# Where the weights of the sixth of seven products are loaded to, in two woven matmul pairs

## The chip, the cores and the metric

The kernel runs on one core of one Trainium2 chip. Its time is device time in microseconds (us), the median of three runs. A profile of one execution, taken by the hardware profiler, is read beside it.

## The reference

Two layers on x of 256 tokens by 2048 channels, in float32: an even one (a linear recurrent unit beside dilated attention) and an odd one (gated linear attention beside a spatial gating unit), then a norm. What matters here is the odd layer's input projection:

```
h = rms_norm(x, norm)
z = h @ w_in                       # 2048 x 7184
q, k, v, a_lr, gc, u, vd, gd = split(z)
yc = rms_norm(gla_chunked(q, k, v, log_a), head_norm) * silu(gc)
yd = spatial_gating(gelu(u), gelu(vd), w_s, b_s, v_norm) * silu(gd)
x = x + concat(yc, yd) @ w_out
```

Every column block of z of 512 columns is a product of 256 x 2048 with 2048 x 512.

## The kernel before, in words

**Products.** float32 values are split in two parts, hi (a cast to float32r on ScalarE, line 138) and lo (the rest, by a subtraction on VectorE, line 73), and each product is three matmuls: hi x hi, hi x lo, lo x hi. A piece of weights of 128 x 1024 (512 KB) comes by one DMA into a buffer, is cast into whi (four buffers) and subtracted into wlo (four buffers), and feeds TensorE. Once the subtraction has run, the raw buffer is free, if nothing else reads it.

**Rings.** Raw buffers come in three rings: `raw` with three buffers, `rx` and `ry` with four each (line 115). Outside the pairs every piece takes the next of the rings in a fixed turn. While `paired[0]` is set, a piece of the stream goes into `raw` alone.

**Pairs.** Two column blocks and two halves of the tokens are a 2 x 2 by 2 x 2 block product over the two halves of the inner dimension. `pair` computes it with seven block products of half size in place of eight. Each is four steps; a step takes one piece and runs six matmuls of 512 columns. Two chains of pieces, x0 (in `rx`) and y0 (in `ry`), are used again and again, changed in place between uses: GpSimd issues DMAs that add other weights to them (line 244). The products run in this order: m12 with x0, m3 with y0, m56 with x0, m7 with y0, m56 again with x0 (the fifth), then the sixth, which adds to m12 and takes four fresh pieces z0, and the seventh, m4, with x0 to which VectorE has added z0 (line 295). In a short loop of six rounds the sixth and seventh products run two rounds apart. The weights z0 are fetched in that loop, into `raw`. In it each z0 buffer stays in use until line 295 has read it.

**Stream.** `weave` puts steps of other products (gates, gd, vd: `Stream`) between the steps of a pair, 14 steps into the first pair (q and k) and 12 into the second (the two blocks of u). A stream step is one piece and twelve matmuls. A task queue (`spawn`, `tick`) feeds the small work of attention, norms and gates in between.

**Queues.** SyncE issues the plain loads in order; an issue that waits for a buffer holds those behind it. The order on each queue is set by the framework's scheduler at build time, from the program's order and the buffers, so a piece's issue may stand far ahead of its use. In the names below a number tells the tiles of one ring apart.

Of the kernel before, what the change touches and what calls it, by code (L numbers as in the profile page):

```python
# [51 lines left out]
def trunk(ctx, tc, x, xt, lead, w_in0, w_out0, w_va, w_in1, w_out1, w_gate, small, dist, cst, w_alpha, w_s,  # L52
# [31 lines left out]
    def mid_tile(shape, name, dtype=F32):  # L84
        return mid.tile(shape, dtype, name=name, tag="mid")
# [13 lines left out]
    def tick(n):  # L99
        for task in list(tasks):  # L100
            task[1] -= n
            if task[1] <= 0:
                wait = next(task[0], None)
                if wait is None:
                    tasks.remove(task)
                else:
                    task[1] = wait
# [11 lines left out]
    def raw_tile(shape, tag=None):  # L119
        if tag is None:  # L120
            tag = "raw"
            if not paired[0]:
                turns.append(turns.pop(0))
                tag = turns[-1]
        return rawp.tile(shape, F32, name=tag, tag=tag, bufs=rings[tag])
# [9 lines left out]
    def parts(raw, n=1024):  # L135
        hi = hip.tile([P, n], F32R, name="whi", tag="whi")
        lo = lop.tile([P, n], F32R, name="wlo", tag="wlo")
        nc.scalar.copy(hi, raw)  # L138
        sub(lo, raw, hi)
        return hi, lo  # L140
# [68 lines left out]
    def piece_of(w, u, i):  # L209
        return w[u + i // 2][:, i % 2 * 1024:i % 2 * 1024 + 1024]  # L210

    def fetch(w, u, i, tag):
        raw = raw_tile([P, 1024], tag)
        nc.sync.dma_start(out=raw, in_=piece_of(w, u, i))
        return raw
# [14 lines left out]
    def pair(w, ua, ub, act, forms, x0, tag):  # L230

        f3, f5, f6, f7 = forms

        def step(ps, a, i, raw, first, u=None):  # L240
            tile_, k0, b = a
            hi, lo = parts(raw)
            if u is not None:
                nc.gpsimd.dma_start(out=raw, in_=piece_of(w, u, i), accum_op=ALU.add)
            for kk in range(2):
                j = 2 * i + kk
                wh, wl = hi[:, kk * 512:(kk + 1) * 512], lo[:, kk * 512:(kk + 1) * 512]
                xh = tile_[:, k0 + j, b * P:(b + 1) * P]
                xl = tile_[:, k0 + j, T + b * P:T + (b + 1) * P]
                nc.tensor.matmul(ps, xh, wh, start=(first and j == 0), stop=False, skip_group_check=not first)  # L250
                nc.tensor.matmul(ps, xh, wl, start=False, stop=False, skip_group_check=not first)  # L251
                nc.tensor.matmul(ps, xl, wh, start=False, stop=(j == 7), skip_group_check=not first)  # L252
                tick(1)

        def run(ps, a, raws, first, u=None):
            for i, raw in enumerate(raws):
                step(ps, a, i, raw, first, u)
                yield

        def bank():  # L260
            return psm.tile([P, 512], F32, name="ps", tag="ps")

        m12, m3, m56, m7 = bank(), bank(), bank(), bank()
        y0 = []
        for i, raw in enumerate(x0):
            y0.append(fetch(w, ub + 2, i, tag))
            step(m12, (act, 0, 0), i, raw, True, ub)
            yield
        s1 = mid_tile([P, 512], "s1")
        nc.scalar.copy(s1, m12)  # L270
        yield from run(m3, f3, y0, True, ub)
        yield from run(m56, f5, x0, True, ub + 2)
        s5 = mid_tile([P, 512], "s5")
        nc.scalar.copy(s5, m56)
        yield from run(m7, f7, y0, True)
        yield from run(m56, f6, x0, False)
        t = mid_tile([P, 512], "t")
        nc.vector.tensor_tensor(out=t, in0=m56, in1=s1, op=ALU.subtract)
        c22 = s1
        nc.vector.tensor_tensor(out=c22, in0=m7, in1=t, op=ALU.add)  # L280
        nc.vector.tensor_tensor(out=t, in0=m3, in1=t, op=ALU.add)
        nc.vector.tensor_tensor(out=s5, in0=s5, in1=c22, op=ALU.subtract)
        m4 = bank()
        z0 = []
        for i in range(6):
            if i < 4:
                z0.append(fetch(w, ua + 2, i, "raw"))
                step(m12, (act, 8, 0), i, z0[i], False)
                yield
            if i > 1:  # L290
                step(m4, (act, 8, 1), i - 2, x0[i - 2], True)
                yield
            if 0 < i < 5:

                tc.keep_in_program_order(nc.vector.tensor_tensor(out=x0[i - 1], in0=z0[i - 1], in1=x0[i - 1],
                                                                 op=ALU.add))
        nc.vector.tensor_tensor(out=s5, in0=m4, in1=s5, op=ALU.add)
        return [m12, s5], [t, c22]
# [528 lines left out]
    paired[0] = True  # L827
    x0 = [fetch(w_in1, 6, i, "rx") for i in range(4)]
    ps, ps_k = weave(pair(w_in1, 6, 10, act2, forms2, x0, "ry"), stream, 14)
    drain()  # L830
    eb, enb, ebl = decays
# [129 lines left out]
    paired[0] = True  # L961
    x0 = [fetch(w_in1, 30, i, "rx") for i in range(4)]
    ud = weave(pair(w_in1, 30, 34, act2, forms2, x0, "ry"), stream, 12)
    paired[0] = False
    for c, ps in enumerate(ud):
# [52 lines left out]
    for s in range(4):  # L1018
        raw = raw_tile([P, 4, 256])
# [118 lines left out]
```

## Time and profile before

| | |
|---|---|
| time, median of 3 runs | 886.4 us (885.5 to 886.6) |
| time of the profiled execution | 889.86 us |
| its span | 888.2 us |
| TensorE busy | 864.7 us, 97% |
| VectorE busy | 590.4 us, 66% |
| ScalarE busy | 513.0 us, 58% |
| mean granted clock of TensorE | 0.99 |

In the names of the profile PE is TensorE, DVE is VectorE, ACT is ScalarE, POOL is GpSimd and SPq is SyncE's queue of DMA issues. Times on the axis count from the span's start. A matmul's duration is longer than the distance to the next one's start, since matmuls are pipelined; the distance of starts tells the rate. The first pair stands at about 539 to 628 us, the second at about 686 to 779.

### The profile page before, as it was taken

To read this page: it belongs to the slowest core of one execution; us is meant where nothing else is said; L and a number is where in the kernel's file an instruction comes from. 1 tells how busy PE (TensorE), PEld (TensorE's weight loads), DVE (VectorE), ACT (ScalarE), POOL (GpSimd) and SP (SyncE) were. 2 spreads that over 40 slices of the span, in tenths; PEclk is the share of its full clock that TensorE was granted. 3 is DMA by queue.
4 is the path that set the end of the run, shared out by engine and by line. 5 is a ranking of instruction groups with operands and counts; after the bars stand their busy time and mean duration, and the time that the engine had idled before them with its cause. 6 is when DMAs were issued, how large, how long until landed. Compare 5 with 4: busy or idle time off the path is not lost.

```text
span 888.2 us, 11858 instructions
## 1 busy us (share of the span) xinstructions
PE 864.7 (97%) x4432; PEld 728.7 (82%) x4432; DVE 590.4 (66%) x848; ACT 513.0 (58%) x751; POOL 31.0 (3%) x48
## 2 busy tenths in 40 slices
PE   8999999999999999999999999997999998899996
PEld 7888888888888888888888988885867886688886
DVE  7577557677576587666555995677645868695652
ACT  6765456676766766554444775653535765564532
POOL 0000000000000000010000002200000220000000
PEclk9999999999999999999999999998999999999999
DMA  9796555555455455565545669965733996665502
GB/s 342 288 389 212 189 192 164 169 174 173 161 178 166 143 181 173 190 210 193 189 127 157 209 199 205 267 218 166 254 127 120 199 266 221 194 232 186 192 3 96
DMA packets 49114, 171.35 MB, mean 193 GB/s; under 512 B 5520, under 2 KB 6032, under 8 KB 48800
## 3 DMA queue, kind: packets, MB, share of 16 engines
q1 hardware_dynamic: 44496, 154.75, 51.2%
q0 software_dynamic: 4416, 15.76, 8.7%
q8 instruction: 35, 0.57, 0.3%
q14 instruction: 23, 0.19, 0.1%
q10 hardware_dynamic: 144, 0.07, 0.0%
HBM read 168.47 MB, written 2.10 MB: 192 GB/s over the span
## 4 chain that ended last, share of the span: by engine, by line
PE 93%; DMA 3%; DVE 2%; ACT 1%; issue 0%; ACTq 0%
PE pc L311 20%; PE ps L146 16%; PE ps L147 16%; PE ps L148 16%; PE pc L310 10%; DMA raw<-in_w_in 3%; PE ps L250 2%; PE ps L252 2%; PE ps L251 2%; DVE wlo L73 1%; PE pc L313 1%; ACT whi L138 1%; PE sc L496 1%; PE gp L580 1%; PE gp L579 1%; DMA sm<-in_small 0%
## 5 line engine op out<-in xcount | busy, mean ns | idle before, releaser
L311 PE MATMUL pc<-act,whi 128*128 128x512 f32 x768 | 269.6, 395 | 0.0
L310 PE MATMUL pc<-act,wlo 128*128 128x256 f32 x720 | 208.7, 290 | 0.0
L73 DVE TENSOR_TENSOR wlo<-rx,whi 128x1024 fp32r<-128x1024 f32 (+2 forms) x117 | 140.3, 1201 | 79.6 <-ACT whi L138 78.5
L138 ACT CAST whi<-rx 128x1024 fp32r<-128x1024 f32 (+1 forms) x114 | 118.8, 1044 | 93.4 <-PE ps L148 55.4
L311 PEld LDWEIGHTS pc<-act,whi 128*128 128x128 f32 x768 | 142.8, 188 | 29.2
L146 PE MATMUL ps<-whi,act 128*128 128x512 f32 (+2 forms) x416 | 159.4, 386 | 5.7 <-ACT whi L138 4.5
L73 DVE TENSOR_TENSOR wlo<-ry,whi 128x1024 fp32r<-128x1024 f32 (+2 forms) x101 | 120.8, 1198 | 66.1 <-ACT whi L138 65.5
L73 DVE TENSOR_TENSOR wlo<-raw,whi 128x1024 fp32r<-128x1024 f32 (+2 forms) x98 | 116.9, 1193 | 62.2 <-ACT whi L138 60.7
L147 PE MATMUL ps<-wlo,act 128*128 128x512 f32 (+2 forms) x416 | 157.7, 379 | 0.3 <-DVE wlo L73 0.3
L148 PE MATMUL ps<-whi,act 128*128 128x512 f32 (+2 forms) x416 | 157.3, 378 | 0.0
L138 ACT CAST whi<-raw 128x1024 fp32r<-128x1024 f32 (+1 forms) x95 | 98.6, 1038 | 93.3 <-PE ps L148 37.9
L138 ACT CAST whi<-ry 128x1024 fp32r<-128x1024 f32 (+1 forms) x99 | 102.8, 1039 | 84.1 <-PE ps L148 52.6
L310 PEld LDWEIGHTS pc<-act,wlo 128*128 128x128 f32 x720 | 136.0, 189 | 2.5 <-DVE wlo L73 0.9
L146 PEld LDWEIGHTS ps<-whi,act 128*128 128x128 f32 x416 | 78.9, 190 | 23.9 <-ACT whi L138 6.1
L146 PE MATMUL ps<-whi,yt 128*128 128x512 f32 (+1 forms) x256 | 97.4, 380 | 0.0
L148 PE MATMUL ps<-whi,yt 128*128 128x512 f32 (+1 forms) x256 | 96.5, 377 | 0.0
L147 PE MATMUL ps<-wlo,yt 128*128 128x512 f32 (+1 forms) x256 | 96.3, 376 | 0.0
L148 PEld LDWEIGHTS ps<-whi,act 128*128 128x128 f32 x416 | 79.3, 191 | 14.4
L147 PEld LDWEIGHTS ps<-wlo,act 128*128 128x128 f32 x416 | 79.4, 191 | 14.1 <-DVE wlo L73 0.7
L148 PEld LDWEIGHTS ps<-whi,yt 128*128 128x128 f32 x256 | 48.2, 188 | 8.9
L147 PEld LDWEIGHTS ps<-wlo,yt 128*128 128x128 f32 x256 | 48.3, 189 | 8.4
L146 PEld LDWEIGHTS ps<-whi,yt 128*128 128x128 f32 x256 | 48.2, 188 | 8.4
(288 smaller groups left out, 923.8 us busy)
## 6 DMA issues: line engine op xcount, KB each, us to landing
raw<-in_w_in SPq DMA_DIRECT2D x76, 512.0 KB, 4.9
ry<-in_w_in SPq DMA_DIRECT2D x66, 512.0 KB, 4.8
rx<-in_w_in SPq DMA_DIRECT2D x66, 512.0 KB, 4.5
rx<-in_w_out SPq DMA_DIRECT2D x23, 512.0 KB, 4.6
ry<-in_w_out SPq DMA_DIRECT2D x23, 512.0 KB, 4.6
raw<-in_w_out SPq DMA_DIRECT2D x18, 512.0 KB, 4.6
rx<-in_w_in POOLq DMA_DIRECT2D x16, 512.0 KB, 9.7
ry<-in_w_in POOLq DMA_DIRECT2D x8, 512.0 KB, 9.7
```

Of the source, the lines that this page charges most:

```text
L73: nc.vector.tensor_tensor(out=o, in0=a, in1=hi.bitcast(F32), op=ALU.subtract)
L138: nc.scalar.copy(hi, raw)
L146: nc.tensor.matmul(ps[b], xh, wh, start=first, stop=False)
L147: nc.tensor.matmul(ps[b], xh, wl, start=False, stop=False)
L148: nc.tensor.matmul(ps[b], xl, wh, start=False, stop=last)
L250: nc.tensor.matmul(ps, xh, wh, start=(first and j == 0), stop=False, skip_group_check=not first)
L251: nc.tensor.matmul(ps, xh, wl, start=False, stop=False, skip_group_check=not first)
L252: nc.tensor.matmul(ps, xl, wh, start=False, stop=(j == 7), skip_group_check=not first)
L310: nc.tensor.matmul(ps[c][:, 1, :], wl, act[:, k, 0:T], start=False, stop=False)
L311: nc.tensor.matmul(ps[c], wh, act[:, k, :], start=(k == 0), stop=(k == KT - 1))
L313: nc.tensor.matmul(ps[c][:, 1, :], wl, act[:, k, 0:T], start=False, stop=False)
L496: nc.tensor.matmul(sc[:, 1:3, :], qk[:, 0, P:T], qk[:, 1, :], start=True, stop=True)
```

## The change

The four fetches of z0 move from the last loop (sixth and seventh product) into the fifth product, one ahead of each of its steps, and their tag is the second chain's ring, `ry`, in place of `raw`. Nothing is computed otherwise. Line numbers grow by 5 for the sums behind the fifth product and by 3 from the additions of line 295 on.

```
--- before.py
+++ after.py
@@ -273,7 +273,12 @@
         s5 = mid_tile([P, 512], "s5")
         nc.scalar.copy(s5, m56)
         yield from run(m7, f7, y0, True)
-        yield from run(m56, f6, x0, False)
+
+        z0 = []
+        for i, raw in enumerate(x0):
+            z0.append(fetch(w, ua + 2, i, tag))
+            step(m56, f6, i, raw, False)
+            yield
         t = mid_tile([P, 512], "t")
         nc.vector.tensor_tensor(out=t, in0=m56, in1=s1, op=ALU.subtract)
         c22 = s1
@@ -281,10 +286,8 @@
         nc.vector.tensor_tensor(out=t, in0=m3, in1=t, op=ALU.add)
         nc.vector.tensor_tensor(out=s5, in0=s5, in1=c22, op=ALU.subtract)
         m4 = bank()
-        z0 = []
         for i in range(6):
             if i < 4:
-                z0.append(fetch(w, ua + 2, i, "raw"))
                 step(m12, (act, 8, 0), i, z0[i], False)
                 yield
             if i > 1:
```

SyncE's queue in the first pair, before: `raw` 5470, 5500, 5513 and 5554 are z0, `ry` 5644, 5708, 5792 and 5873 are stream pieces used behind the pair, and the other `raw` are stream pieces in the pair.

```order
L132 DMA raw_5398<-in_w_in1 128x1024
L132 DMA ry_5644<-in_w_in1 128x1024
L132 DMA raw_5436<-in_w_in1 128x1024
L132 DMA ry_5708<-in_w_in1 128x1024
L132 DMA ry_5792<-in_w_in1 128x1024
L214 DMA raw_5470<-in_w_in1 128x1024
L132 DMA ry_5873<-in_w_in1 128x1024
L132 DMA raw_5482<-in_w_in1 128x1024
L214 DMA raw_5500<-in_w_in1 128x1024
L214 DMA raw_5513<-in_w_in1 128x1024
L132 DMA raw_5525<-in_w_in1 128x1024
L214 DMA raw_5554<-in_w_in1 128x1024
```

The same place now: `ry` 5386, 5418, 5430 and 5460 are z0.

```order
L132 DMA raw_5400<-in_w_in1 128x1024
L214 DMA ry_5386<-in_w_in1 128x1024
L132 DMA raw_5442<-in_w_in1 128x1024
L214 DMA ry_5418<-in_w_in1 128x1024
L214 DMA ry_5430<-in_w_in1 128x1024
L132 DMA raw_5488<-in_w_in1 128x1024
L214 DMA ry_5460<-in_w_in1 128x1024
L132 DMA raw_5527<-in_w_in1 128x1024
L132 DMA raw_5566<-in_w_in1 128x1024
L132 DMA raw_5605<-in_w_in1 128x1024
L132 DMA ry_5644<-in_w_in1 128x1024
L132 DMA raw_5732<-in_w_in1 128x1024
```

The z0 issues took the places of the `ry` issues for later, the stream's next `raw` pieces took those of z0, and the first `ry` piece for later stands behind all four of z0.

VectorE in the first pair, before, from the operation that ends the fifth product's sums: `rx` 5040 is the first piece of x0, enb, ebl and eb are scaled with the pair's results.

```order
L282 TENSOR_TENSOR s5_5304<-s5_5304,s1_5142 128x512
L837 SCALAR_TENSOR_TENSOR enb_4714<-t_5464,rs1_4488,enb_4714 128x512
L837 SCALAR_TENSOR_TENSOR ebl_4715<-t_5464,rs1_4488,ebl_4715 128x512
L837 SCALAR_TENSOR_TENSOR enb_4714<-s1_5142,rs1_4488,enb_4714 128x512
L73 TENSOR_TENSOR wlo_5528<-raw_5525,whi_5527 128x1024
L73 TENSOR_TENSOR wlo_5544<-rx_5040,whi_5543 128x1024
L295 TENSOR_TENSOR rx_5042<-raw_5500,rx_5042 128x1024
L837 SCALAR_TENSOR_TENSOR ebl_4715<-s1_5142,rs1_4488,ebl_4715 128x512
L841 MEMSET ebl_4715 64x512
```

The same place now:

```order
L287 TENSOR_TENSOR s5_5304<-s5_5304,s1_5142 128x512
L73 TENSOR_TENSOR wlo_5530<-raw_5527,whi_5529 128x1024
L73 TENSOR_TENSOR wlo_5546<-rx_5040,whi_5545 128x1024
L298 TENSOR_TENSOR rx_5042<-ry_5418,rx_5042 128x1024
L73 TENSOR_TENSOR wlo_5557<-ry_5460,whi_5556 128x1024
L73 TENSOR_TENSOR wlo_5569<-raw_5566,whi_5568 128x1024
L73 TENSOR_TENSOR wlo_5585<-rx_5042,whi_5584 128x1024
L298 TENSOR_TENSOR rx_5044<-ry_5430,rx_5044 128x1024
L836 SCALAR_TENSOR_TENSOR eb_4713<-ps_5048,rs1q_4492,eb_4713 128x512
```

The three scalings of line 837 (now 840) that stood ahead of the stream piece's subtraction stand behind it, and the subtraction of the last z0 piece comes right behind the second addition.

## Rows read from the trace of the kernel before

**Rows 1.** the page, busy time of each engine, TensorE's entry

```profile
PE 864.7 (97%) x4432; PEld 728.7 (82%) x4432; DVE 590.4 (66%) x848; ACT 513.0 (58%) x751; POOL 31.0 (3%) x48
```

**Rows 2.** busy time by stretches: length, busy time of each engine, clock, DMA

```profile
600.50:628.20 27.70, 22.50 (x83) 17.05 (x83) 20.42 (x21) 12.78 (x13) 0.00 (x0) 0.88 0.60 201
...
743.70:778.90 35.20, 27.52 (x109) 21.14 (x108) 27.08 (x35) 19.15 (x21) 0.00 (x0) 0.95 0.53 167
...
594.80:617.00 22.20, 17.00 (x63) 12.40 (x62) 16.96 (x20) 7.54 (x8) 0.00 (x0) 0.88 0.41 126
...
710.00:740.00 30.00, 30.00 (x134) 24.87 (x133) 21.77 (x24) 19.70 (x20) 5.36 (x7) 1.00 1.04 295
```

**Rows 3.** TensorE's waits between 590 and 800: total, times, longest

```profile
PE ps L250 <- ACT whi L138: 7.2, 5, 3.6
PE ps L146 <- ACT whi L138: 4.5, 3, 2.3
```

**Rows 4.** ScalarE's timeline in the tails: start, duration, line, idle before

```profile
600.60 1.05 ACT L138 CAST whi<-raw 128x1024 fp32r<-128x1024 f32 x1 [3.39 <-DMA raw<-in_w_in]
...
611.48 1.04 ACT L138 CAST whi<-raw 128x1024 fp32r<-128x1024 f32 x1 [3.96 <-DMA raw<-in_w_in]
...
762.62 1.04 ACT L138 CAST whi<-raw 128x1024 fp32r<-128x1024 f32 x1 [7.79 <-DMA raw<-in_w_in]
```

**Rows 5.** SyncE's queue of issues in the tails

```profile
569.09 0.33 SPq L132 DMA_DIRECT2D ry<-in_w_in  x1
...
573.16 2.17 SPq L132 DMA_DIRECT2D ry<-in_w_in  x2
...
587.11 5.42 SPq L214 DMA_DIRECT2D raw<-in_w_in  x2
...
721.77 0.33 SPq L132 DMA_DIRECT2D ry<-in_w_in  x1
...
728.57 0.33 SPq L132 DMA_DIRECT2D ry<-in_w_out  x1
```

**Rows 6.** TensorE's timeline in the tails

```profile
600.32 0.39 PE L252 MATMUL ps<-whi,act 128*128 128x512 f32 x1
...
627.98 0.39 PE L148 MATMUL ps<-whi,act 128*128 128x512 f32 x1
...
742.35 0.39 PE L250 MATMUL ps<-whi,sums 128*128 128x512 f32 x1
...
743.71 0.39 PE L250 MATMUL ps<-whi,act 128*128 128x512 f32 x1
...
778.71 0.39 PE L148 MATMUL ps<-whi,act 128*128 128x512 f32 x1
```

**Rows 7.** DMA issues, 555 to 640, then at 721, 728 and 727; last, landing

```profile
ry<-in_w_in SPq DMA_DIRECT2D x7, 512.0 KB, 7.6
...
ry<-in_w_in SPq DMA_DIRECT2D x1, 512.0 KB, 9.1
...
ry<-in_w_out SPq DMA_DIRECT2D x1, 512.0 KB, 13.7
...
raw<-in_w_in SPq DMA_DIRECT2D x1, 512.0 KB, 13.0
```

**Rows 8.** VectorE's timeline in the tails

```profile
598.98 0.68 DVE L282 TENSOR_TENSOR s<-s,s 128x512 f32<-128x512 f32 x1
599.58 0.75 DVE L837 SCALAR_TENSOR_TENSOR enb<-t,rs,enb 128x512 f32<-128x512 f32 x1
...
601.68 1.23 DVE L73 TENSOR_TENSOR wlo<-raw,whi 128x1024 fp32r<-128x1024 f32 x1
602.82 1.22 DVE L73 TENSOR_TENSOR wlo<-rx,whi 128x1024 fp32r<-128x1024 f32 x1
...
747.72 1.20 DVE L295 TENSOR_TENSOR rx<-raw,rx 128x1024 f32<-128x1024 f32 x1
...
753.13 1.22 DVE L73 TENSOR_TENSOR wlo<-raw,whi 128x1024 fp32r<-128x1024 f32 x1
```

More of the change, by code (lines that the diff above doesn't have):

```diff
@@ L275, in pair @@
         yield from run(m7, f7, y0, True)
-        yield from run(m56, f6, x0, False)
+        z0 = []
+        for i, raw in enumerate(x0):
+            z0.append(fetch(w, ua + 2, i, tag))
+            step(m56, f6, i, raw, False)
+            yield
         t = mid_tile([P, 512], "t")
@@ L283, in pair @@
         m4 = bank()
-        z0 = []
         for i in range(6):
             if i < 4:
-                z0.append(fetch(w, ua + 2, i, "raw"))
                 step(m12, (act, 8, 0), i, z0[i], False)
```

## The prediction

> Single times are microseconds on the axis of the profiled execution of before. A "z piece" is one of the four 512 KB pieces of weights of the sixth product, which VectorE then adds to x0 for the seventh; z0 to z3 in order.
>
> **What bounds the kernel now.** I read the page's engine table first, then busy time by stretches, then TensorE's waits, then the timelines of the engines that it waits for. TensorE is busy for 864.7 of 888.2 us [rows 1], so almost any change elsewhere is hidden. The stretches tell where it is not: 710 to 740 is full at clock 1.00, but from 600.5 to 628.2, the tail of the first pair, it is busy for 22.50 of 27.70 us at a mean granted clock of 0.88, and from 743.7 to 778.9, the tail of the second, for 27.52 of 35.20 us at 0.95 [rows 2]. The waits of that part of the program are nearly all for ScalarE's casts of line 138, 7.2 and 4.5 us [rows 3], and the casts in their turn stood waiting for a transfer into raw: 3.39, 3.96 and 7.79 us in the rows shown [rows 4]. In both tails the plain ring (three buffers) carries the stream's pieces and the z pieces, and SyncE sends a piece only when a buffer is free: issues at 569.09 and 721.77 go to the other ring ry for work that lies beyond the pair, while two z pieces follow from 587.11 on, 5.42 us for the two [rows 5].
>
> What a tail loses: TensorE starts a 512-column matmul every 0.227 us where it waits for nothing (a step of six begins at 742.35, the next step at 743.71) [rows 6]. From 600.55 (the last matmul of z2's step starts at 600.32) to 628.21 (the last one of the step starts at 627.98) there are 78 such matmuls by the code (6 for a step of the pair, 12 for one of the stream), 17.7 us, and four transposes of 128 columns, a quarter of a slot to a whole one each, 0.2 to 0.9 us, of which I take 0.7. So 18.4 us of work took 27.7: **9.2 us lost**, 5.2 of them idle and 4.0 at the lower clock and at restarts. In the second tail, from 743.71 to 778.94 (last start 778.71), there are 96 matmuls (21.8 us) and 12 of 256 columns (half a slot to a slot, 1.4 to 2.7 us; I take 2.0): 23.8 us of work in 35.2, **11.5 us lost**, 7.7 of them idle. Together 20.7 us is all that this change can give back.
>
> **Part 1: z pieces go into ry.** No byte, cast, subtraction, product or addition is added or removed. Eight issues of 512 KB change their ring and their place. SyncE's queue, in the two order fences, shows the trade: where before sent a ry piece for later, after sends a z piece; where before sent a z piece into raw, after sends the stream's next piece. A ry buffer comes free by the same subtraction of the fourth product as before, so the slots fall at the same times: z0 of the first pair at 569.09, of the second at 721.77 [rows 5]. Landing: the ry pieces of the first stretch took 7.6 us in the median; in the second the first ry piece took 9.1, the last one 13.7, and the piece in raw between them 13.0, so that one lands at 740.2 [rows 7]. So z0 of the second pair lands at 730.9 and z3 (slot 728.57 [rows 5]) at 742.3; the cast of z3 cannot be wanted before 748. Where the casts waited for 3 to 8 us they now wait for none. The DMA engines are full there (share 1.04 from 710 to 740 [rows 2]), but the bytes in these slots are those of before, so I cost the earlier issue at nothing; if that cover went, the price is how much later than 748 z3 lands.
>
> The Trainium skill, DMA: Bandwidth & Descriptors, section Issuing engines are not separate DMA queues, speaks against the change: transfers of all queues run on the same 16 DMA engines and interleave, so z pieces sent into a full stretch should slow the additions that GpSimd's queue does there for x0. The trace agrees that the stretch is full; the sum stays, since the slots held the same bytes before.
>
> **Part 2: what is late next is VectorE.** With pieces on time, ScalarE casts as TensorE frees the four buffers of whi, and VectorE's own order decides. I walk it with durations from rows: a subtraction or a 1024-wide addition follows the one before by 1.14 us (601.68, 602.82) and lasts 1.22, the operation behind a 512-wide one starts 0.60 after it (598.98, 599.58), and line 837's lasts 0.75 [rows 8]; a cast lasts 1.05 [rows 4].
>
> First pair. Up to 599.58 nothing changes (the operations up to L282, now L287, stand as they did). Then the three scalings of line 837, which before stood ahead of the stream's subtraction, go behind it. So the subtraction of the stream piece ends at 600.8 instead of 602.9; of x0's first sum at 601.9; addition for x0's second 603.1; subtraction of z3 604.2; next stream piece 605.4; second sum 606.5; third addition 607.6; two scalings to 608.9; third sum (cast 607.7 to 608.7) 610.1; stream piece 611.2; fourth addition 612.4; two scalings; fourth sum 614.8. TensorE, at 0.227, needs these at 600.8, 603.6, 605.0, 606.3, 609.0, 610.4, 611.8 and 614.5 and goes on at 619.0 after the step that before ended at 628.21: it loses 0.1 at the first and covers the last with a step of the stream. Gain **9.2 us**, with VectorE within 0.3 us of TensorE in three places.
>
> Second pair. VectorE has a block that does not go away: from the addition at 747.72 to the subtraction of z2 at 753.13, 5.4 us, mostly the norm of the stream's vf [rows 8]. Its opening operation waits for the end of the fifth product (743.71 on TensorE [rows 6]) and for the stream piece's subtraction (cast from 742.6, when the stream's step ahead of 742.35 has freed whi; subtraction to 744.85), so the addition behind it now begins at 745.45 instead of 747.72 and the subtraction of z2 ends at 752.1 instead of 754.3. TensorE, with no wait for z0, z1 and the stream piece (24 matmuls from 743.71), reaches z2 at 749.15, does what needs no subtraction, and stands for some 1.4 us until 752.1. From there each subtraction is there 0 to 1 us ahead until the last sum of x0, for which it waits another 0.7 us. The step that before ended at 778.94 ends at 769.5. Gain **9.4 us** of the 11.5.
>
> **Part 3: behind the pairs.** The ry pieces for the work behind are now sent when the addition has read z: first at 596.6 (pair one) and 746.7 (pair two), the others between 603 and 612 and between 755 and 763. TensorE needs them from 614 and 764 on, one every 2.7 us. Even a landing of 13.7 us leaves the first ones in time and makes a later one about 1.5 us late; at the usual landing they cost nothing. The work behind is unchanged in order and dense, so a gain stays a gain to the end.
>
> **Sum.** 9.2 + 9.4 = 18.6 us of the profiled execution's 889.9 us, giving 871.3 there; the median of the runs shown is 3.5 us below that execution, so 886.4 - 18.6 = 867.8. Each walk has three or four places without slack, and a hand-over is some 0.05 to 0.1 us, so I give back 0.35 us for each tail: **868.5 us**.
>
> **Rivals.**
> *No wait left at all:* VectorE's places turn out covered; 886.4 - 20.7 = 865.7. Against it is the 5.4 us block of the second pair [rows 8]. 10%.
> *VectorE becomes the bound:* the additions and scalings stand in front of subtractions, so the lag of 0.1 to 0.7 us grows from step to step. Nine steps in each tail, 0.2 to 0.6 us each, take 4 to 11 us from the gain: 872 to 879. For it speaks that VectorE has no idle time left between 594.8 and 617 in my walk; against it, that in before it was busy for 16.96 of these 22.2 us [rows 2], so that 5.2 are there to be used. 21%.
> *The clock falls once more:* the 1.4 us wait in the second tail drops it. A fall cost at most the 4.0 us that the first tail lost without being idle: 868.5 to 872.5, inside the range of the forecast and of the case before. The Trainium skill, Perfetto Trace Analysis, section Matmul Optimizations, says that power follows utilization and matmuls should come back to back; the rows agree, with a granted clock of 0.88 in a tail with many waits and 1.00 in the full stretch.
> *The DMA engines decide:* the z pieces are issued early and land late all the same. If z2 and z3 of both pairs land only as in before, the waits stay where they are: 884.6 to 888.2, no change. Against it are the landings of the same slots [rows 7]. 5%. The section of the Trainium skill named under part 1 is the rule behind this case.
> *Slower:* SyncE sends in order. A z piece that waits for y0's buffer holds the stream's raw piece behind it. If a buffer came free one 4.1 us step late (the gap between the issues at 569.09 and 573.16 [rows 5]), four raw pieces of each pair would be late by it, 8 x 4.1 = 33 us against 20.7: 899. It decides as soon as y0's subtractions lag the stream's; in before the same slots waited for the same subtractions and the casts behind them found their data. 4%.
>
> **How the numbers follow.** The forecast with its own range of 866.5 to 871.5 has 55%, the others as given, 5% lies between 879 and 884.6. Range for 8 in 10: 865.0 to 876.5. What can be told from no change is 0.2%, 1.8 us: faster 0.91, the same 0.05, slower 0.04.
>
> **What would show it.** Right: no wait of a cast in the tails for a transfer into raw or ry; TensorE's waits between 590 and 800 at 2 to 4 us, for VectorE's line 73 instead of ScalarE; clock 1.00 in the first tail; VectorE nearly full there; the z issues at about 569 to 579 and 722 to 729. Wrong: casts that wait for ry in the sixth or seventh product; SyncE waiting in front of a z issue with raw buffers free; waits on rx or ry in the 15 us behind a pair; a gain in one tail only.

## The result, and the profile after

The changed kernel takes **869.97 us** in the median of four runs (869.87 to 871.58), the kernel before 886.5 beside it (885.5 to 887.2); the ratio is 0.9819 with a 95% interval of 0.9802 to 0.9836. The forecast was 868.5, in a range of 865.0 to 876.5. The profiled execution took 870.03 us, with a span of 868.3.

The page's engine table, TensorE's row, which answers to [rows 1]:

```profile
PE 856.9 (99%) x4432; PEld 724.4 (83%) x4432; DVE 589.0 (68%) x848; ACT 513.1 (59%) x751; POOL 32.6 (4%) x48
```

The same instructions, 7.8 us less busy time in a span 19.9 us shorter: most of what went (12.1 us) was idle time, the rest mainly matmuls that ran at the lower clock before.

Busy time by stretches of the changed kernel: length, busy time of the five engines, TensorE's granted clock, DMA share, GB/s. The rows answer to [rows 2]: first tail, second tail, the first tail's dense part, the full stretch ahead of the second tail. Its axis lies some 1.98 us earlier at the first pair and 11.09 us earlier at the second than that of before.

```profile
598.56:616.97 18.41, 18.41 (x84) 14.94 (x82) 18.21 (x21) 9.54 (x10) 0.00 (x0) 1.00 0.85 289
732.62:758.79 26.17, 25.04 (x109) 20.07 (x108) 25.69 (x34) 17.24 (x19) 0.00 (x0) 1.00 0.66 221
592.80:615.00 22.20, 22.20 (x101) 18.09 (x100) 22.20 (x25) 11.95 (x13) 0.00 (x0) 1.00 0.72 240
698.90:728.90 30.00, 30.00 (x134) 24.86 (x133) 21.67 (x24) 20.74 (x22) 5.36 (x7) 1.00 1.05 296
```

The first tail fell from 27.66 to 18.41 us: TensorE never stops, the clock is 1.00, and VectorE is busy for 18.21 of 18.41 us. The second fell from 35.23 to 26.17 us, with 1.1 us idle and VectorE at 25.69. The full stretch carries the same traffic as before (1.05 against 1.04). The rows of before with these lengths stand under before_again.

TensorE's waits between 580 and 800 (waiting line, who released it, total, times, longest); they answer to [rows 3]:

```profile
PE ps L251 <- DVE wlo L73: 1.1, 1, 1.1
```

The 7.2 and 4.5 us for ScalarE's casts are gone; before, the same line 251 waited for 1.2 us there. SyncE's queue in the changed kernel (start, duration, line), for [rows 5]:

```profile
567.10 0.33 SPq L214 DMA_DIRECT2D ry<-in_w_in  x1
...
571.18 2.17 SPq L214 DMA_DIRECT2D ry<-in_w_in  x2
...
576.62 0.33 SPq L214 DMA_DIRECT2D ry<-in_w_in  x1
...
710.68 3.53 SPq L214 DMA_DIRECT2D ry<-in_w_in  x3
...
717.48 0.33 SPq L214 DMA_DIRECT2D ry<-in_w_in  x1
```

On the axis of before these are 569.1, 573.2, 578.6, 721.8 and 728.6: the z pieces took exactly the slots in which ry pieces stood. Landing of the first and the last z piece of the second pair (queue, count, size, us from issue to landing), for [rows 7]:

```profile
ry<-in_w_in SPq DMA_DIRECT2D x1, 512.0 KB, 8.8
...
ry<-in_w_in SPq DMA_DIRECT2D x1, 512.0 KB, 13.9
```

The last, issued at 717.48, is there at 731.4, which is 742.5 on the axis of before (742.3 had been worked out). ScalarE's timeline shows the casts of the four z pieces (ry): two from 727.76, one at 733.94, one at 738.31, for [rows 4]:

```profile
727.76 2.03 ACT L138 CAST whi<-ry 128x1024 fp32r<-128x1024 f32 x2
...
733.94 1.04 ACT L138 CAST whi<-ry 128x1024 fp32r<-128x1024 f32 x1
735.68 1.05 ACT L138 CAST whi<-rx 128x1024 fp32r<-128x1024 f32 x1 [0.70 <-DVE rx L298]
...
738.31 1.05 ACT L138 CAST whi<-ry 128x1024 fp32r<-128x1024 f32 x1 [0.62 <-ACT whi L138]
744.52 1.05 ACT L138 CAST whi<-rx 128x1024 fp32r<-128x1024 f32 x1 [5.16 <-DVE rx L298]
```

No cast in the tail waits for a transfer; the longest wait in these rows, 5.16 us, is for VectorE's addition into x0 (line 298). From 590 to 790 one cast still waits for a transfer, for 0.6 us and ahead of the tail (722.25). The last z piece had lain there for 6.9 us when it was cast.

VectorE's timeline in the second tail, for [rows 8], and TensorE's at the one stop left:

```profile
734.38 1.19 DVE L298 TENSOR_TENSOR rx<-ry,rx 128x1024 f32<-128x1024 f32 x1
735.49 1.06 DVE L823 TENSOR_SCALAR vf<-vf,mv,rv 128x256 f32<-128x256 f32 x3
736.46 0.69 DVE L825 TENSOR_TENSOR vf<-vf,vn 128x512 f32<-128x512 f32 x1
...
739.78 1.22 DVE L73 TENSOR_TENSOR wlo<-ry,whi 128x1024 fp32r<-128x1024 f32 x1
```

```profile
738.97 1.02 PE L958 MATMUL s_ps<-vf,wst 128*128 128x256 f32 x4
741.05 0.50 PE L251 MATMUL ps<-wlo,act 128*128 128x512 f32 x1 [1.06 <-DVE wlo L73]
```

The block from the addition to z2's subtraction is 5.4 us long as before, and TensorE stands until 741.05, for 1.06 us by the trace.

### The profile page after: what moved, and what is told of

Read it like the earlier page. It is cut to its first block, busy times and chain, and to the rows that moved or that the text cites. A ratio compares the mean times of both kernels' runs of the same rounds, so it can differ in the third digit from the quotient of the medians.

```text
span 868.3 us, 11869 instructions
## 1 busy us (share of the span) xinstructions
PE 856.9 (99%) x4432; PEld 724.4 (83%) x4432; DVE 589.0 (68%) x848; ACT 513.1 (59%) x751; POOL 32.6 (4%) x48
## 4 chain that ended last, share of the span: by engine, by line
PE 97%; DVE 1%; DMA 0%; ACT 0%; issue 0%; ACTq 0%; DVEq 0%
PE pc L314 20%; PE ps L146 16%; PE ps L147 16%; PE ps L148 16%; PE pc L313 10%; PE ps L251 3%; PE ps L252 3%; PE ps L250 3%; PE pc L316 1%; PE sc L499 1%; PE gp L583 1%; PE gp L582 1%; PE pt_ps L517 0%; PE ps L1034 0%; PE ps L1033 0%; PE ps L1032 0%
## 5 line engine op out<-in xcount | busy, mean ns | idle before, releaser
L73 DVE TENSOR_TENSOR wlo<-ry,whi 128x1024 fp32r<-128x1024 f32 (+2 forms) x109 | 130.4, 1198 | 67.9 <-ACT whi L138 67.2
L138 ACT CAST whi<-ry 128x1024 fp32r<-128x1024 f32 (+1 forms) x107 | 111.1, 1040 | 86.6 <-PE ps L148 52.1
L146 PE MATMUL ps<-whi,act 128*128 128x512 f32 (+2 forms) x416 | 157.8, 382 | 1.0 <-DVE la_s L472 0.9
L148 PE MATMUL ps<-whi,act 128*128 128x512 f32 (+2 forms) x416 | 155.6, 374 | 0.0
L73 DVE TENSOR_TENSOR wlo<-raw,whi 128x1024 fp32r<-128x1024 f32 (+2 forms) x90 | 106.8, 1187 | 49.3 <-ACT whi L138 48.1
L138 ACT CAST whi<-raw 128x1024 fp32r<-128x1024 f32 (+1 forms) x87 | 90.3, 1038 | 61.9 <-PE ps L148 35.4
L146 PEld LDWEIGHTS ps<-whi,act 128*128 128x128 f32 x416 | 78.0, 188 | 18.2 <-issue 3.2
L148 PEld LDWEIGHTS ps<-whi,act 128*128 128x128 f32 x416 | 78.2, 188 | 14.0
```

Of the source, the lines that this page charges most:

```text
L73: nc.vector.tensor_tensor(out=o, in0=a, in1=hi.bitcast(F32), op=ALU.subtract)
L146: nc.tensor.matmul(ps[b], xh, wh, start=first, stop=False)
L148: nc.tensor.matmul(ps[b], xl, wh, start=False, stop=last)
```

## The experiments

The ratios are to the kernel before, run on the same chip. The theory that they test: z pieces sat in plain buffers until VectorE's addition had read them, so the stream's pieces were sent late; in the second chain's ring they hold nothing up; what remains is VectorE.

**before_again**, the kernel before, unchanged, for a second profile.

> The kernel before, unchanged, for a second profile. The profiled gain is 19.9 us of span, the medians differ by 16.5. Theory: the 3.4 us between them belong to that one execution of before: 2.0 us stand ahead of the pairs, where its first matmuls ran at half clock (starts 0.43 us apart from 7.4 to 10.8), the rest in the tails. Expected: 885.5 to 887.2 us; if the first matmuls run at full clock (0.23 apart), the first pair begins 1.5 to 2.5 us earlier; the tails again lose 8 to 9.5 and 10 to 11.5 us. Rival: the start is alike and the tails lose 3 us less than in the first profile.

Measured 886.1 us, span 884.4, against the first profile's 888.2. TensorE's start in the first profile, then in the second (start, duration):

```profile
7.77 0.63 PE L148 MATMUL ps<-whi,act 128*128 128x512 f32 x1
8.20 0.63 PE L147 MATMUL ps<-wlo,act 128*128 128x512 f32 x1
```

```profile
7.66 0.40 PE L148 MATMUL ps<-whi,act 128*128 128x512 f32 x1
7.89 0.39 PE L147 MATMUL ps<-wlo,act 128*128 128x512 f32 x1
```

The first ran its opening matmuls 0.43 us apart until 10.8, at a granted clock of 0.50 from 8 on, the lower of the two levels (1.2 GHz); the second ran them 0.23 apart, at 1.00. The two tails in the second profile:

```profile
598.92:625.67 26.75, 20.38 (x84) 14.78 (x84) 19.83 (x20) 12.67 (x13) 0.00 (x0) 1.00 0.60 198
741.17:775.15 33.98, 27.47 (x109) 20.84 (x108) 26.99 (x35) 19.34 (x21) 0.00 (x0) 0.95 0.52 173
```

The same two in the first profile:

```profile
600.55:628.21 27.66, 22.46 (x84) 17.05 (x84) 20.38 (x21) 12.78 (x13) 0.00 (x0) 0.88 0.61 201
743.71:778.94 35.23, 27.55 (x109) 21.14 (x108) 27.12 (x35) 19.14 (x21) 0.00 (x0) 0.95 0.53 167
```

So the first tail took 26.75 us where it had taken 27.66, and the second 33.98 where it had taken 35.23. In the first profile matmuls stood 0.43 us apart from 614.9 to 618.3, after a stop of 2.29 us, and again from 765.7 to 768.7, after one of 3.56 us; in the second the same stops were 1.62 and 2.70 us, and behind both the matmuls stand 0.23 apart:

```profile
760.85 0.50 PE L250 MATMUL ps<-whi,act 128*128 128x512 f32 x1 [2.70 <-ACT whi L138]
...
762.46 0.39 PE L252 MATMUL ps<-whi,act 128*128 128x512 f32 x1
762.68 0.40 PE L250 MATMUL ps<-whi,act 128*128 128x512 f32 x1
```

But the second profile has a spell of its own elsewhere in the second tail: behind a stop of 2.48 us that ends at 750.11 its granted clock is 0.50 until 753. So the mean clock of that tail is 0.95 in both, and the 1.25 us are in the stops (6.5 us idle against 7.7). In the first tail the second profile keeps the clock at 1.00, but stands longer (6.4 us idle against 5.2). Of the 3.8 us between the two spans 1.6 arose ahead of the first tail and 2.2 in the tails (0.9 and 1.25). How long the stops are, and where a spell at the lower clock follows one, differs from execution to execution.

**ring_only**, the kernel before with the ring alone changed; the fetch stays in the last loop.

```
-                z0.append(fetch(w, ua + 2, i, "raw"))
+                z0.append(fetch(w, ua + 2, i, tag))
```

> Only the ring of the z pieces is changed (ry in place of raw); their fetches stay in the last loop. SyncE's queue and the other engines' orders come out as in the changed kernel. Theory (the ring alone makes the gain, the place of the fetch in the code does nothing): 869.5 to 870.5 us, no difference from the change. Rival (the early fetch is needed): part of the gain is missing, 874 us or more.

Measured 870.07 us (870.03 to 871.28), ratio 0.9823 (0.9805 to 0.984), the same single wait of 1.1 us. The ring makes the whole gain. Where the fetch stands in the code does nothing: the z issues of the first pair stand at 567.35, 571.43 and 576.87, 0.25 us later than in the changed kernel, as its whole first tail does. Not run is a fourth plain buffer with the z pieces left in `raw`; whether that would have done as much stays open.

**second_only**, the change in the second pair alone; the first fetches as before.

```
+            if early:
+                z0.append(fetch(w, ua + 2, i, tag))
...
+                if not early:
+                    z0.append(fetch(w, ua + 2, i, "raw"))
...
-    ps, ps_k = weave(pair(w_in1, 6, 10, act2, forms2, x0, "ry"), stream, 14)
+    ps, ps_k = weave(pair(w_in1, 6, 10, act2, forms2, x0, "ry", False), stream, 14)
```

> The change in the second pair alone; the first pair fetches z into raw as before. Theory (two tails, each its own gain, 9.2 us for the first): 878 to 880 us, tail of the first pair with its casts waiting for raw as before, tail of the second with one wait of 1.1 us for VectorE. Rival (the tails depend on each other, since the first leaves the rings and VectorE in another state): 874 or less, or 883 or more.

Measured 878.27 us (877.67 to 879.44), ratio 0.9913 (0.9895 to 0.9931). TensorE's waits between 580 and 800:

```profile
PE ps L146 <- ACT whi L138: 3.3, 3, 1.4
PE ps L251 <- DVE wlo L73: 1.8, 2, 1.1
PE ps L250 <- ACT whi L138: 1.6, 2, 1.4
```

By the medians the second pair gives 886.25 - 878.27 = 8.0 us, which leaves 8.3 to the first (878.27 - 869.97). The rows say the same without that subtraction: the second tail takes 26.15 us (740.57 to 766.72) as in the changed kernel (26.17), and the first, whose pieces come as before, 26.17 us (598.90 to 625.07) against 18.41, 7.8 us more, with its waits for ScalarE still there. So the tails don't depend on each other. The first tail's 26.17 us, at a clock of 1.00, are a third length for the same work, beside 27.66 and 26.75.

**norm_late**: the block in VectorE put off.

```
-        yield 2
+        yield 2 if c == 0 else 26
```

> The changed kernel with the norm of the stream's second vf block put off by 24 ticks, so that on VectorE it stands behind the subtractions of z2, x0's first sum and the stream piece. Theory (the 1.4 us that TensorE stands in the second tail are this block's): 868.3 to 869.2 us, no wait of TensorE for line 73 of over 0.5 us in the second tail. Rival (VectorE is full there, and the block delays a later subtraction by as much): 869.7 to 870.5 us, the wait moved to the second or third sum of x0.

Measured 871.49 us (870.33 to 871.88), ratio 0.9834 (0.9816 to 0.9851). The theory expected 868.3 to 869.2 and fell. The rival was right in that the wait moves; its time of 869.7 to 870.5 holds for one of the five runs (870.33), and the others are above it. TensorE's waits between 580 and 800 and the single stops:

```profile
PE ps L146 <- ACT whi L138: 0.6, 2, 0.3
PE ps L251 <- DVE wlo L73: 0.2, 1, 0.2
```

```profile
747.84 0.73 PE L146 MATMUL ps<-whi,act 128*128 128x512 f32 x2 [0.26 <-ACT whi L138]
...
753.26 0.50 PE L251 MATMUL ps<-wlo,act 128*128 128x512 f32 x1 [0.16 <-DVE wlo L73]
...
756.48 0.74 PE L146 MATMUL ps<-whi,act 128*128 128x512 f32 x2 [0.32 <-ACT whi L138]
```

z2's stop is gone, three smaller ones stand in its place, and the second tail is 26.52 us long (734.01 to 760.53) against 26.17. The rest of the 1.5 us is the start, by which the second tail begins 1.39 us later than in the changed kernel (734.01 against 732.62): this profile, too, began with matmuls 0.43 apart, until 9.6. The granted clock reads 1.00 in its rows there, so that the clock is the cause isn't shown here.

```profile
7.47 0.63 PE L147 MATMUL ps<-wlo,act 128*128 128x512 f32 x1
7.90 0.63 PE L148 MATMUL ps<-whi,act 128*128 128x512 f32 x1
```

**no_norm**: that block left out altogether, with the longer start of warm14 (below), which takes 870.23 us by itself.

```
         yield 2
+        if c:
+            return
```

> The kernel with 14 matmuls on zeros at the start (870.2 us), and the norm of the stream's second vf left out: four scalings and two products, 2.5 us of VectorE's time at the head of the second tail, put nowhere else (the output isn't the reference's by that). Theory: what is left of the second tail's loss is VectorE's amount of work there; without the block nothing of 2.5 us is to be done and nothing slows the subtractions beside it, so TensorE's 1.1 us wait for line 73 goes and the tail falls from 26.2 to 24.5 to 25.0 us: 868.9 to 869.3 us. Rival: the next waits on VectorE's additions or ScalarE's casts take over at once, as when the norm was put off: 869.9 to 870.3 us, with waits of 0.2 to 0.5 us behind z2.

Measured 869.16 us (868.98 to 869.43), ratio 0.981 (0.9797 to 0.9824): 1.07 us less than with the norm, within the theory's 868.9 to 869.3. Between 732.6 and 759 TensorE is busy throughout and VectorE no longer:

```profile
732.60:759.00 26.40, 26.40 (x116) 21.22 (x116) 23.77 (x28) 18.76 (x21) 0.00 (x0) 1.00 0.71 241
```

So what was left in the second tail is VectorE's amount of work, not the place of the block: put off it moves the wait, left out it takes the wait away.

**norm_pool**: the norm is done by GpSimd.

```
+        eng = nc.gpsimd if c else nc.vector
...
-                nc.vector.tensor_scalar(out=t, in0=t, scalar1=mv[:, 4 * c + at, 0:1], scalar2=rv[:, at:at + 1],
+                eng.tensor_scalar(out=t, in0=t, scalar1=mv[:, 4 * c + at, 0:1], scalar2=rv[:, at:at + 1],
...
-            nc.vector.tensor_mul(vf[c][:, b, :], vf[c][:, b, :], vn[:, c, :])
+            eng.tensor_tensor(out=vf[c][:, b, :], in0=vf[c][:, b, :], in1=vn[:, c, :], op=ALU.mult)
```

> The changed kernel, but the norm of the stream's second vf (its four scalings of 256 columns and two products of 512, together 4 x 0.33 + 2 x 0.60 = 2.5 us of VectorE's 5.4 us block in the second tail) is done by GpSimd, which has nothing else to do there. Theory: the 1.4 us for which TensorE stands at z2 is VectorE's amount of work, not the place of the block; with 2.5 us of it gone the second tail falls from 26.2 us to about 24.2 to 24.8, so 868.0 to 868.9 us where TensorE starts at full clock. Rival 1: GpSimd works on the same memory as VectorE and slows VectorE's subtractions beside it by a tenth or more; over the 15 us or so that GpSimd needs that is 1.5 us or more, and the time stays at 870 or goes above it. Rival 2: the wait only moves behind the block again, as it did when the norm was put off, and the second tail keeps 26.2 to 26.5 us.

Measured 871.17 us (869.8 to 871.54), ratio 0.9836 (0.9823 to 0.985): no gain. GpSimd's timeline, and VectorE's beside it:

```profile
734.90 7.14 POOL L824 TENSOR_SCALAR vf<-vf,mv,rv 128x256 f32<-128x256 f32 x3 [19.00 <-DVE rv L330]
742.00 1.59 POOL L826 TENSOR_TENSOR vf<-vf,vn 128x512 f32<-128x512 f32 x1
743.58 4.29 POOL L824 TENSOR_SCALAR vf<-vf,mv,rv 128x256 f32<-128x256 f32 x1
```

```profile
739.88 1.22 DVE L73 TENSOR_TENSOR wlo<-raw,whi 128x1024 fp32r<-128x1024 f32 x1
741.02 1.42 DVE L298 TENSOR_TENSOR rx<-ry,rx 128x1024 f32<-128x1024 f32 x1
742.36 2.31 DVE L73 TENSOR_TENSOR wlo<-ry,whi 128x1024 fp32r<-128x1024 f32 x1
744.60 1.21 DVE L73 TENSOR_TENSOR wlo<-rx,whi 128x1024 fp32r<-128x1024 f32 x1
```

The subtraction at 742.36, which begins inside GpSimd's product of 742.00 to 743.59, takes 2.31 us in place of 1.22, and TensorE waits 0.48 us for it at 744.73. GpSimd's fourth scaling takes 4.29 us beside VectorE's subtractions, more than its first three took each (7.14 / 3). The Trainium skill, SBUF — State Buffer, section SBUF: two separate sides, says that the two engines share a pair of ports as an exclusive lock, held for a whole instruction, also against a VectorE operation with two inputs in SBUF. The row of the product agrees: the subtraction ends 1.09 us late, near the 1.23 us that the product still ran. The rows of the scalings don't settle it: the subtraction at 744.60 takes 1.21 us inside the 4.29 us of the fourth scaling, so there it is GpSimd that is slow.

**warm14**: five more matmuls on zeros ahead of the program.

```
-WARM = 9
+WARM = 14
```

> The changed kernel with 14 instead of 9 matmuls of 128 columns on zeros ahead of the program. Theory: the runs differ by 1.4 to 1.9 us because in some of them TensorE does its first eight or so matmuls of 512 columns at half the granted clock (starts 0.43 us apart instead of 0.23), after a pause of about 0.9 us between the zeros and the first real matmul; with five more matmuls (0.2 us each, or 1.0 us) that pause is filled, all runs start at full clock and lie within 0.3 us of 870.0. Rival 1: the zeros run into the time at which the first data are there, and the first real matmul starts later: 870.2 to 871. Rival 2: whether the clock has risen by then is a matter of time since the start alone, and some runs still lie at 871.4 to 871.6.

Measured 870.23 us in the median of four runs, 870.18 to 870.62, ratio 0.9829 (0.9815 to 0.9842). With no_norm and pool_warm, which start in the same way, 13 runs lie within 0.6 us of each other for each kernel; at 9 the 18 runs of after, ring_only, norm_late and norm_pool lie between 869.8 and 871.9, nine of them up to 870.33 and nine from 871.17 on. Theory and the first rival both hold a part: the spread is gone, and the start costs 0.2 us. TensorE stands for 0.56 us until 6.97, when it has one real matmul behind it and the changed kernel three, and the second tail begins 0.44 us later (733.06).

**pool_warm**: both edits together, as a version that could beat the changed kernel.

> The changed kernel with both edits: 14 matmuls on zeros at the start, and the second vf's norm on GpSimd. Theory: the longer start removes the runs at half clock and costs 0.2 us; the norm on GpSimd gives 0.4 to 0.5 us although it slows two of VectorE's subtractions: 869.6 to 870.0 us in all runs. Rival: GpSimd's work beside VectorE's gives back as much as it takes, 870.1 to 870.4 us, and the spread is that of the runs at 14 matmuls.

Measured 870.46 us (870.33 to 870.9), ratio 0.9826 (0.9813 to 0.984). The rival holds in the main (870.1 to 870.4 expected): it beats nothing.

**raw2**: the changed kernel with two plain buffers in place of three.

```
-    rings = {"raw": 3, "rx": 4, "ry": 4}
+    rings = {"raw": 2, "rx": 4, "ry": 4}
```

> The changed kernel with two buffers instead of three in the plain ring, in the whole program. Theory: what cost 18 to 21 us before was that z pieces sat in the plain ring until VectorE's addition had read them; a ring that only the stream uses needs few buffers, so the two tails keep 18.4 and 26.2 us within half a microsecond each, and whatever is lost is lost elsewhere, where the plain ring runs on its own: 870 to 874 us. Rival: the tails were short because three buffers stand ready for the stream; with two the casts of the stream's pieces wait for transfers again, in the tails as well, 2 to 4 us in each: 874 to 880 us with waits of TensorE for ScalarE between 590 and 780.

Measured 875.2 us (874.03 to 876.69), ratio 0.9885 (0.9871 to 0.9898). By the median it is in the rival's range, by the place of the loss it is the theory. TensorE's waits over the whole span, the two largest behind the start, and ScalarE's cast behind the larger:

```profile
PE ps L146 <- ACT vf L808: 4.9, 1, 4.9
...
PE ps L251 <- DVE wlo L73: 1.1, 1, 1.1
```

```profile
731.19 1.04 ACT L138 CAST whi<-raw 128x1024 fp32r<-128x1024 f32 x1 [7.49 <-DMA raw<-in_w_in]
732.25 1.28 ACT L808 ACT_TABLE_LOAD   x1
733.55 1.27 ACT L808 ACTIVATE vf<-ps,rs 128x512 f32<-128x512 f32 x2
```

The first tail has no wait and takes 18.40 us (598.71 to 617.11) against 18.41. The second has only the known 1.1 us, and from that stop to its end it takes 17.72 us (748.53 to 766.25) as in the changed kernel (17.74, 741.05 to 758.79). In this profiled execution, the longest of the four runs (876.69), the second tail begins at 740.11 instead of 732.62, and nearly all of that is lost in one place ahead of it, in the stretch that is full of transfers: ScalarE stands 7.5 us for a plain piece, two activations stand behind its cast, and TensorE waits 4.9 us for the bank that they read; behind that stop matmuls are 0.43 us apart, at a granted clock of 0.50, until 738. So in the tails two buffers are enough for the stream; in the full stretch the third is worth 5 us by the medians. That I had priced at 0 to 4.

## Why the prediction was right, and what was mis-sized

**What bounds it, and part 1.** Right. The z pieces took the slots of the ry pieces to 0.1 us, landed in 8.8 to 13.9 us in the second pair (9.1 to 13.7 from [rows 7]) and in 8.6 in the median in the first (7.6), and no cast waits for them. GpSimd's addition that is issued beside the first z piece of the second pair landed in 10.9 us, as long as before (10.9). ring_only shows that the ring is the whole cause, second_only that each pair has its own share. DMA as the bound, the rival of 5%, is excluded: the last z piece lay there 6.9 us early. SyncE's head-of-line rival is excluded by the queue: no issue stands late.

**Part 2, first pair.** Right to 0.1 us: the end worked out as 619.0 came at 618.95 on the axis of before, VectorE busy for 18.21 of 18.41 us, as walked. VectorE as a growing lag (21%) did not occur: the order of the instructions gives each subtraction just before TensorE needs it.

**Part 2, second pair.** Right in mechanism: TensorE stands 1.4 us, as worked out, between the end of its earlier work and 741.05 (the four matmuls from 738.97 are done by 739.64, if they take 0.67 us as such four do from 751.43 to 752.10; the trace counts 1.06 of it as idle). The end worked out as 769.5 came at 769.88, a gain of 9.06 instead of 9.4. That it is so near is in part luck: the second wait, 0.7 us for the last sum of x0, did not come, so the 2 to 4 us of waits for line 73 that were to be the sign came out at 1.1; and the matmuls took 24.76 us (26.17 less the 1.41 of the stop) instead of 23.8. That is 1 us above the sized work, where 0.35 had been given back for hand-overs; the first tail took nothing above it (18.41 against 18.4). The block is also not mostly the norm: the norm is 2.5 of its 5.4 us, the rest is the addition and the pair's own sums. The stop did not lower the clock: 1.00 over the whole tail. That rival is thus excluded for this stop; the stops of 2.29 and 3.56 us in before, of 2.48 in before_again and of 4.88 in raw2 had a granted clock of 0.50 behind them, while the one of 2.70 in before_again had not, so the length of the stop alone doesn't decide it.

**The step that was mis-sized is the sum.** It took the losses of one profiled execution (9.2 and 11.5 us) and subtracted the gains from a median that lay 3.5 us below that execution. But a part of those 3.5 us were the same losses: before_again has 0.9 and 1.25 us less in the two tails. With its tails the gains are 26.75 - 18.41 = 8.34 and 33.98 - 26.17 = 7.81, together 16.15 us, and 886.4 - 16.15 = 870.25 against 869.97 measured; with the first profile's they are 9.25 and 9.06, 18.3, near the 18.6 of the sum. What was counted twice is 2.2 us, more than the error of 1.5 us; the 0.7 us given back for hand-overs covered a part. This rests on one more profile, whose execution of 886.1 us lies near the median; the first tail of second_only, 26.17 us, points the same way.

**Part 3.** Right: behind neither pair does a cast wait for a transfer, and none of TensorE's waits between 580 and 800 stands there. Between the tails the gain shrank by 0.15 us (115.65 us against 115.50), which the prediction had at nothing.

**No wait left at all** (865.7) is excluded by the 1.1 us stop behind VectorE's block; no_norm prices that block's norm at 1.1 us.

## What to carry to other kernels

A buffer ring is loaded by how long its pieces are held, not by how many pass through it: pieces that wait for a later addition belong in a ring whose own user is idle then. Where a gain is taken from the losses of one profiled execution, subtract it from that execution's time, or profile twice: the waits and the spells at the lower clock are not the same in each run. When the waits are gone, look which engine is full in that stretch; here, moving work about on the full engine, or to one whose instructions held it up, moved the wait and not the end.

## What had not been expected of the hardware

The start decides 1.4 to 1.6 us: in the first profile of before and in that of norm_late TensorE's first matmuls are 0.43 us apart for about 3 us, in the others 0.23. The granted clock is 0.50 there in before, but reads 1.00 in norm_late. That the same is behind the upper half of the 18 times at 9 matmuls on zeros is inferred from their distance and from the 13 times at 14, which don't show it; but for norm_late's profiled run those have no trace. And a GpSimd product of 1.59 us lengthened VectorE's subtraction beside it from 1.22 to 2.31 us (in norm_pool, and again in pool_warm), nearly by the GpSimd operation's remaining length (742.36 to 743.59 is 1.23 us).
